# Masked softmax on one core: the transfer of the lengths behind an iota, and two waits on GpSimd moved

## The chip, the core and the metric

The kernel runs on one core of a Trainium2 chip. A core has five engines with instruction streams of their own: TensorE (PE, with its weight loads as PEld), VectorE (DVE), ScalarE (ACT), GpSimd (POOL) and SyncE (SP). They meet through semaphores: an instruction waits until a semaphore has reached a value, and raises one when it is done. Sixteen DMA engines move data between the chip's memory (HBM) and the on-chip buffer (SBUF). A transfer is issued by SyncE, ScalarE or GpSimd, and each of the three has its own DMA queue; the sixteen engines serve all queues.

The metric is the device time of one execution in microseconds (us), as the median of several runs. Beside it stands one profiled execution, whose trace gives the start and the end of each instruction.

## The reference

The input x has 16 batches of 8 heads with 256 x 256 float32 each. Every batch has a length between 128 and 255. Each row is a softmax over its first `length` columns; the columns behind it are zero.

```python
for b in range(batch):
    length = lengths[b]
    masked = x[b, :, :, :length].copy()
    masked = masked - np.max(masked, axis=-1, keepdims=True)
    exp_masked = np.exp(masked)
    result[b, :, :, :length] = exp_masked / np.sum(exp_masked, axis=-1, keepdims=True)
```

## The kernel before

A batch is 2048 rows of 256 columns, 2 MB. It lies in SBUF as 128 partitions with 16 rows each, and `xt` has eight such slots. The batches are worked through in sixteen positions; the first position is batch 1, and `batch_of` gives the batch of a position. A *half* is 8 of the 16 rows of each partition, 1 MB.

The work on one position runs through four engines. A load brings the batch into its slot. VectorE applies the mask to the columns from 128 on (`mask`, L248): the minimum of x and a bound that is hugely positive inside the length and hugely negative behind it. The bound is put together from two small tiles: `down`, made from a count of the columns (the *first bound*, L231), and `len_s`, the lengths of all batches on every partition (the *second bound*, L239). Both raise the semaphore `s_v`, so that `s_v` is 1 after the first and 2 after the second. ScalarE then takes the exponential in place (L374 for a quarter of the batch at once, L377 row by row with the sums). VectorE sums that quarter (`total`, L269), takes reciprocals (L279) and multiplies (`divide`, L282), half by half. SyncE stores the result in pieces (L154). The row's maximum is not subtracted; a check at the end (L317 to L328) would start a slow second pass if a sum were out of range.

VectorE's program interleaves two positions: after the first half of one has been divided it masks the next, then divides the second half and sums a quarter of the next. ScalarE runs through the slots in order.

The opening is this. GpSimd makes the count of the columns (`iota_i`, L181), a row and a column of ones, and two small memsets (`seed`) that raise the store semaphores. ScalarE issues the transfer of the sixteen lengths (L142) as its first act, then loads its table for the exponential (L361). SyncE issues the load of the first position in two halves (L145); VectorE masks each half when it has landed. VectorE makes the first bound when the iota is there, casts the lengths to `len_b` when they have landed (L236), TensorE spreads them over the partitions (L216), and VectorE makes the second bound from that (L239). GpSimd waits for `s_v` = 2 (L188). Then it fills the columns from 160 on of one slot with zeros (`fill(ahead)`, L191), issues the loads of positions 1 to 3 (L196), waits for the lengths, and fills three more slots.

Later loads are issued by GpSimd in a loop (L168), each only as wide as the length of its batch needs, in steps of eight columns, which is why slots have to be filled. Each waits for the store that frees its slot and for the last load but one.

A transfer's instruction stands in its engine's stream, and its packets go through that engine's DMA queue. SyncE's stores wait for the divided half (`s_out`), and from position 2 on also for the stores two positions earlier.

Of the kernel before, what the change touches and what calls it, by code (L numbers as in the profile page):

```python
# [21 lines left out]
def kernel(  # L22
# [6 lines left out]
    nc = tc.nc  # L29
# [20 lines left out]
    def batch_of(pos):  # L50
        return pos + 1 if pos < ahead - 1 else {ahead - 1: 15, 15: 0}.get(pos, pos)
# [54 lines left out]
    with tc.tile_critical(no_gpsimd_drain=True):  # L106
# [8 lines left out]
        s_iota = sem("s_iota")  # L115
        s_fill = sem("s_fill")
        s_v = sem("s_v")
# [21 lines left out]
            )  # L139


        nc.scalar.dma_start(out=word64, in_=lengths[None, :]).then_inc(s_word, 16)  # L142
        for h in range(2):
            s = slice(h * half, (h + 1) * half)
# [40 lines left out]
        nc.gpsimd.memset(ones_c, 1.0).then_inc(s_ones, 1)  # L185
        for par in range(2):
            nc.gpsimd.memset(seed[:, par : par + 1], 0.0).then_inc(s_st[par], 128)  # L187
        nc.gpsimd.wait_ge(s_v, 2)  # L188

        def fill(b):  # L190
            nc.gpsimd.memset(xt[:, b, :, low:], 0.0).then_inc(s_fill, 1)  # L191


        fill(ahead)
        for b in range(1, ahead):
            nc.gpsimd.dma_start(out=xt[:, b], in_=x_f[batch_of(b)]).then_inc(  # L196
                s_sw[b - 1] if b < 3 else s_ld[2], 16
            )
# [239 lines left out]
```

## Time and profile before

| what | value |
|---|---|
| median of 3 runs | 154.57 us (154.54 to 154.61) |
| span of the profiled execution | 152.8 us |
| VectorE busy | 134.6 us, 88% |
| ScalarE busy | 95.1 us, 62% |
| GpSimd busy | 21.3 us, 14% |
| moved by DMA | 61.57 MB, mean 403 GB/s |
| HBM read, written | 27.98 MB, 33.55 MB |

The span goes from the first to the last instruction of the profiled execution; the run's time takes in what lies around it. Busy times are those of instructions on an engine: an issue by SyncE or ScalarE isn't counted. In the lists that follow, L142 is line 142 of the kernel before; a row of the timeline gives the start from the span's beginning, the duration, the engine (with a q where the engine's sequencer issues a transfer), the line, the operation, what is written and what is read, and in brackets how long the engine stood idle and what ended that. A packet counts in the window in which it starts, which is why a share can be somewhat above 1 or 100%.

### The profile page before, as it was taken

Reading aid. Unit: us, or ns where it says so; the run is one execution under the profiler, and the core shown is the slowest. Engines: PE = TensorE matmul, PEld = TensorE weight load, DVE = VectorE, ACT = ScalarE, POOL = GpSimd, SP = SyncE. Lnnn points to the kernel's source line nnn. Section 1 sums busy time; section 2 is a strip of 40 time slices with the busy share of each in tenths; the row PEclk is TensorE's granted clock in tenths of the full one; section 3 lists DMA queues with packets and bytes.
Section 4 is the critical chain, followed back from the end, with each engine's and each line's share of the span. In section 5 each row is a group of like instructions: output and inputs, shape, how many; then the busy total and the mean of one; then the engine's idle time right before and its main releaser. Section 6 shows DMA issues by size and latency. Waiting matters only on the chain.

```text
span 152.8 us, 818 instructions
## 1 busy us (share of the span) xinstructions
PE 0.3 (0%) x2; PEld 0.2 (0%) x2; DVE 134.6 (88%) x107; ACT 95.1 (62%) x402; POOL 21.3 (14%) x29
## 2 busy tenths in 40 slices
PE   0000000000000000000000000000000000000000
PEld 0000000000000000000000000000000000000000
DVE  1369999999999999999999999999999999999500
ACT  3096699339394967859393939577593939395000
POOL 4962110030303020030300220302000000000000
DMA  4999999999999999999999999999999999999994
GB/s 107 420 446 433 401 435 347 421 445 420 394 397 422 405 421 411 411 409 405 419 411 418 408 399 419 408 410 423 417 421 419 413 420 422 435 435 442 429 410 187
DMA packets 10646, 61.57 MB, mean 403 GB/s; under 512 B 898, under 2 KB 1010, under 8 KB 7058
## 3 DMA queue, kind: packets, MB, share of 16 engines
q1 hardware_dynamic: 5904, 35.65, 56.7%
q0 software_dynamic: 4736, 25.89, 41.9%
q14 instruction: 4, 0.03, 0.1%
q10 hardware_dynamic: 2, 0.00, 0.0%
HBM read 27.98 MB, written 33.55 MB: 403 GB/s over the span
## 4 chain that ended last, share of the span: by engine, by line
DVE 87%; DMA 5%; issue 1%; SPq 0%; PE 0%
DVE xt L282 48%; DVE xt L248 23%; DVE row_sum L269 12%; DMA xt<-in_x_dram 5%; DVE inv_sum L279 3%; DVE ends L317 0%; SPq L145 0%; DVE bad L320 0%; PE count L218 0%; DVE redo L328 0%; SPq L433 0%; SPq L106 0%
## 5 line engine op out<-in xcount | busy, mean ns | idle before, releaser
L377 ACT ACTIVATE xt<-xt 128x256 f32<-128x256 f32 x192 | 76.6, 400 | 0.2 <-DVE xt L248 0.2
L282 DVE TENSOR_TENSOR xt<-xt,inv_sum 128x2048 f32<-128x2048 f32 x32 | 73.3, 2292 | 1.1
L374 ACT ACTIVATE xt<-xt 128x1024 f32<-128x1024 f32 x16 | 16.9, 1056 | 42.8 <-DVE xt L248 42.8
L248 DVE SCALAR_TENSOR_TENSOR xt<-down,len_s,xt 128x2048 f32<-128x2048 f32 (+1 forms) x17 | 37.7, 2219 | 5.0 <-DMA xt<-in_x_dram 5.0
L377 ACT ACTIVATION_READ_ACCUMULATOR xt<-xt 128x1 f32 x192 | 35.9, 187 | 0.0
L168 POOL DMA_DIRECT2D xt<-in_x_dram x12 | 13.2, 1104 | 84.0 <-DMA xt<-in_x_dram 62.3
L269 DVE TENSOR_REDUCE row_sum<-xt 128x4 f32<-128x1024 f32 x16 | 19.4, 1210 | 0.0
L279 DVE RECIPROCAL inv_sum<-row_sum 128x8 f32<-128x8 f32 x32 | 6.3, 198 | 0.5
L191 POOL MEMSET xt<- 128x1536 f32 x4 | 5.4, 1398 | 1.1 <-DVE len_s L239 1.1
L361 ACT ACT_TABLE_LOAD x1 | 1.3, 1283 | 1.6 <-SPq L106 1.6
L196 POOL DMA_DIRECT2D xt<-in_x_dram x3 | 1.8, 590 | 0.0
L231 DVE TENSOR_SCALAR down<-iota_i 128x256 f32<-128x256 int32 x1 | 0.3, 300 | 1.6 <-POOL iota_i L181 1.6
L317 DVE TENSOR_REDUCE ends<-inv_sum 128x1 f32<-128x256 f32 x2 | 0.7, 408 | 0.0
L236 DVE CAST len_b<-word 1x16 bf16<-1x16 int32 x1 | 0.2, 164 | 0.4 <-DMA word<-in_lengths_dram 0.4
L239 DVE TENSOR_SCALAR len_s<-len_f 128x16 f32<-128x16 f32 x1 | 0.2, 176 | 0.3 <-PE len_f L216 0.3
L218 PE MATMUL count<-bad,ones_c 128*1 128x3 bf16 x1 | 0.2, 165 | 140.8 <-DVE bad L320 140.8
L181 POOL IOTA iota_i<- 128x256 int32 x1 | 0.3, 331 | 0.6 <-SPq L106 0.6
L328 DVE TENSOR_REDUCE redo<-count 1x1 f32<-1x3 f32 x1 | 0.1, 150 | 0.3 <-PE count L218 0.3
L320 DVE TENSOR_SCALAR bad<-ends 128x1 bf16<-128x1 f32 x3 | 0.3, 150 | 0.0
L187 POOL MEMSET seed<- 1x1 f32 x2 | 0.2, 225 | 0.0
L218 PEld LDWEIGHTS count<-bad,ones_c 128*1 128x1 bf16 x1 | 0.1, 79 | 140.8 <-DVE bad L320 140.8
L361 ACT ACTIVATE warm<-const-float32-0.0 128x1 f32<-128x1 f32 x1 | 0.2, 204 | 0.0
(10 smaller groups left out, 1.1 us busy)
## 6 DMA issues: line engine op xcount, KB each, us to landing
out_dram<-xt SPq DMA_DIRECT2D x20, 1024.0 KB
xt<-in_x_dram POOLq DMA_DIRECT2D x4, 2048.0 KB, 16.3
out_dram<-xt SPq DMA_DIRECT2D x15, 512.0 KB
xt<-in_x_dram POOLq DMA_DIRECT2D x3, 1728.0 KB, 16.7
out_dram<-xt SPq DMA_DIRECT2D x2, 2048.0 KB
xt<-in_x_dram POOLq DMA_DIRECT2D x2, 1600.0 KB, 16.0
xt<-in_x_dram POOLq DMA_DIRECT2D x2, 1280.0 KB, 14.7
xt<-in_x_dram SPq DMA_DIRECT2D x2, 1024.0 KB, 6.4
```

The source lines that it names most:

```text
L168: nc.gpsimd.dma_start(out=xt[:, slot, :, :w], in_=x_n[:, b, :, :w]).then_inc(s_sw[par], 16)
L191: nc.gpsimd.memset(xt[:, b, :, low:], 0.0).then_inc(s_fill, 1)
L196: nc.gpsimd.dma_start(out=xt[:, b], in_=x_f[batch_of(b)]).then_inc(s_sw[b - 1] if b < 3 else s_ld[2], 16)
L218: nc.tensor.matmul(count, lhsT=ones_c, rhs=bad, start=True, stop=True).then_inc(s_count, 1)
L248: return nc.vector.scalar_tensor_tensor(out=t, in0=down[:, None, lo:hi].to_broadcast([P, s.stop - s.start, hi - lo]), scalar=len_s[:, batc ...
L269: nc.vector.tensor_reduce(out=row_sum[:, b % slots, :lump], in_=xt[:, b % slots, :lump, :], op=ALU.add, axis=AX,).then_inc(s_exp[0], 1)
L279: step(nc.vector.reciprocal(out=inv_sum[:, b, s], in_=row_sum[:, b % slots, s]))
L282: nc.vector.tensor_tensor(out=t, in0=t, in1=inv_sum[:, b, s, None].to_broadcast([P, half, seq_k]), op=ALU.mult,).then_inc(s_out, 1)
L317: step(nc.vector.tensor_reduce(out=ends[:, k : k + 1], in_=values, op=op, axis=AX))
L361: nc.scalar.activation(out=warm, in_=nc.const_aps.tensor(0.0, (P, 1), F32), func=EXP)
L374: nc.scalar.activation(out=e, in_=e, func=EXP).then_inc(s_lump, 1)
L377: ins = nc.scalar.activation(out=e, in_=e, func=EXP, accum_out=row_sum[:, slot, j : j + 1])
```

## The change

ScalarE waits for the iota before it issues the transfer of the lengths. GpSimd's wait for `s_v` = 2 is split: the first fill waits for `s_v` = 1, and the three loads behind it for `s_v` = 2. Nothing is added to or taken from the computation; the lines below the first added one move by one, those below the second by two.

```diff
+        nc.scalar.wait_ge(s_iota, 1)
         nc.scalar.dma_start(out=word64, in_=lengths[None, :]).then_inc(s_word, 16)
...
             nc.gpsimd.memset(seed[:, par : par + 1], 0.0).then_inc(s_st[par], 128)
-        nc.gpsimd.wait_ge(s_v, 2)
+        nc.gpsimd.wait_ge(s_v, 1)

         def fill(b):
             nc.gpsimd.memset(xt[:, b, :, low:], 0.0).then_inc(s_fill, 1)


         fill(ahead)
+        nc.gpsimd.wait_ge(s_v, 2)
         for b in range(1, ahead):
             nc.gpsimd.dma_start(out=xt[:, b], in_=x_f[batch_of(b)]).then_inc(
                 s_sw[b - 1] if b < 3 else s_ld[2], 16
             )
```

## The prediction

> **What bounds the kernel now.** I read the page first: which engine is busy, what the DMA queues took, and the chain that ended last.
>
> ```profile
> span 152.8 us, 818 instructions
> ...
> q1 hardware_dynamic: 5904, 35.65, 56.7%
> q0 software_dynamic: 4736, 25.89, 41.9%
> ...
> DVE 87%; DMA 5%; issue 1%; SPq 0%; PE 0%
> ```
>
> Two things claim the time. The chain names VectorE (DVE), 87%. But the two data queues together took 56.7 + 41.9 = 98.6% of what sixteen DMA engines have in the whole span. And the shares of the chain add up to some 93%, so it doesn't reach the end. The chain in order of time shows where it stops:
>
> ```profile
> 1.58 7.66 DMA xt<-in_x_dram
> ...
> 143.74 0.15 DVE redo L328
> ```
>
> It stops at 143.89, 8.9 us before the span does. So I read the busy share of the DMA engines stage by stage (columns: stretch, length, busy time of PE, PEld, DVE, ACT, POOL, clock, DMA share, GB/s), and what SyncE waited for at the end:
>
> ```profile
> 1.00:2.17 1.17, 0.00 (x0) 0.00 (x0) 0.30 (x1) 0.52 (x1) 0.70 (x5) 1.00 0.00 0
> 2.17:3.40 1.23, 0.17 (x1) 0.10 (x1) 0.34 (x2) 0.96 (x2) 0.35 (x1) 1.00 1.13 240
> 3.40:8.46 5.06, 0.00 (x0) 0.00 (x0) 1.28 (x1) 0.68 (x1) 5.06 (x6) 1.00 1.00 421
> 8.46:126.50 118.04, 0.00 (x0) 0.00 (x0) 115.83 (x85) 82.23 (x352) 14.95 (x14) 1.00 1.02 413
> 126.50:142.46 15.96, 0.00 (x0) 0.00 (x0) 15.75 (x13) 10.71 (x50) 0.00 (x0) 1.00 1.02 433
> 142.46:151.30 8.84, 0.17 (x1) 0.08 (x1) 1.14 (x7) 0.00 (x0) 0.00 (x0) 1.00 0.93 393
> ```
>
> ```profile
> SPq L433 <- DMA out_dram<-xt: 4.2, 1, 4.2
> ```
>
> Nothing moves before 2.17; then the DMA engines are full until about 151, and SyncE's last act is to wait 4.2 us for a store. The kernel is a DMA pipe of 149 us that is never empty, with VectorE almost as full beside it. So a microsecond in which the DMA engines stand idle comes back at the end, and a late VectorE costs nothing while stores are queued. How much may it be late? After the last store has been issued (142.83) the store queue still moves this much, in the view of the DMA queues:
>
> ```profile
> q1 hardware_dynamic: 379, 3.33, 78.6%
> ```
>
> 3.33 MB less the last store's own 1.05 is 2.28 MB of older stores, at 433 GB/s 5.3 us of slack.
>
> The change touches the opening, so that is what I read next, in order of time (start, duration, instruction, idle time before it). First ScalarE's issue and the first of SyncE's two, then VectorE, then GpSimd, and the first store:
>
> ```profile
> 1.09 0.52 ACTq L142 DMA_DIRECT2D word<-in_lengths_dram  x1
> 1.14 0.39 SPq L145 DMA_DIRECT2D xt<-in_x_dram  x1
> ```
>
> ```profile
> 1.61 0.30 DVE L231 TENSOR_SCALAR down<-iota_i 128x256 f32<-128x256 int32 x1 [1.61 <-POOL iota_i L181]
> 2.31 0.16 DVE L236 CAST len_b<-word 1x16 bf16<-1x16 int32 x1 [0.40 <-DMA word<-in_lengths_dram]
> 2.82 0.18 DVE L239 TENSOR_SCALAR len_s<-len_f 128x16 f32<-128x16 f32 x1 [0.35 <-PE len_f L216]
> 6.46 1.28 DVE L248 SCALAR_TENSOR_TENSOR xt<-down,len_s,xt 128x1024 f32<-128x1024 f32 x1 [3.47 <-DMA xt<-in_x_dram]
> ...
> 14.16 2.34 DVE L248 SCALAR_TENSOR_TENSOR xt<-down,len_s,xt 128x2048 f32<-128x2048 f32 x1
> ```
>
> ```profile
> 3.05 1.39 POOL L191 MEMSET xt<- 128x1536 f32 x1 [1.11 <-DVE len_s L239]
> 4.37 1.76 POOL L196 DMA_DIRECT2D xt<-in_x_dram  x3
> ```
>
> ```profile
> 14.27 0.34 SPq L154 DMA_DIRECT2D out_dram<-xt  x1
> ```
>
> And the DMA queues in short windows: q1 is SyncE's queue, q10 ScalarE's, q0 GpSimd's, and a row gives packets, MB, share. From 1.98 to 2.00 come the lengths' two packets, 0.89 us after their issue at 1.09:
>
> ```profile
> q10 hardware_dynamic: 2, 0.00, 6.2%
> ```
>
> From 2.17 to 5.20 SyncE's queue runs alone and moves nearly the whole first half of x:
>
> ```profile
> q1 hardware_dynamic: 119, 0.97, 99.4%
> ```
>
> From 4.30 to 7.66 it is still alone, though GpSimd issued its first load at 4.37:
>
> ```profile
> q1 hardware_dynamic: 188, 1.41, 99.4%
> ```
>
> From 7.66 to 8.46 GpSimd's packets come in as the two halves run out, and from 8.46 to 9.30 the last two, small packets of the halves follow:
>
> ```profile
> q0 software_dynamic: 20, 0.33, 95.5%
> q1 hardware_dynamic: 24, 0.08, 25.1%
> ...
> q1 hardware_dynamic: 2, 0.00, 0.1%
> ```
>
> From 14.20 to 17.90 GpSimd's queue is alone, though SyncE issued its store at 14.27:
>
> ```profile
> q0 software_dynamic: 107, 1.57, 103.7%
> ```
>
> And GpSimd's first load lands 9.3 us after its issue, at 13.7:
>
> ```profile
> xt<-in_x_dram POOLq DMA_DIRECT2D x1, 2048.0 KB, 9.3
> ```
>
> So in both places where one queue was running and another began, the newcomer's packets waited: 3.3 us (4.37 to 7.66) and 3.6 us (14.27 to 17.90), where an issue into idle engines took 1.03 us (1.14 to 2.17).
>
> **The change part by part.** *The lengths.* ScalarE's issue moves from 1.09 to when the iota is done. VectorE's first bound waits for the same iota and starts at 1.61, so I take 1.61. Behind the wait on ScalarE stand its table load and the exponentials, which need nothing before the first mask at 6.46: a delay of 0.52 there is hidden. Unhindered, the lengths would be cast 1.22 us after the issue, as now (1.09 to 2.31): at 2.83. But their packets would come at 1.61 + 0.89 = 2.50, and by then (from 2.17) the DMA engines are in the first half of x. No row shows so small a transfer in a busy engine. Bounds: it overtakes, cast at 2.83; or it waits until both halves are out at 8.46, and with the 0.32 from packets to cast (1.99 to 2.31) the cast is at 8.78. I take the middle case, nearest to the two newcomers above: it waits for about what is queued when it comes, the first half of x, out at 5.2, and the cast starts at 5.5.
>
> *The fill.* It moves ahead, behind the first bound, which ends at 1.91: from about 2 to 3.4 in place of 3.05 to 4.44. VectorE and the DMA engines don't need it; its 1.39 us is hidden behind the wait for the lengths, and no longer stands ahead of the loads. If that cover were gone it would delay the loads by at most these 1.39.
>
> *The loads.* They now wait for the second bound: the cast plus 0.69 (2.31 to its end at 3.00) plus 0.05 (3.00 to GpSimd at 3.05). With the cast at 5.5: issued at 6.24 in place of 4.37, 1.87 later. Behind them on GpSimd stand three more fills and the later loads, first needed at 14.5.
>
> *Does that leave the DMA engines idle?* How soon GpSimd's load reaches an idle engine isn't shown. From below: its issue, 1.76 / 3 = 0.59 (SyncE's took 0.39), and then what SyncE's needed from its issue's end at 1.53 to 2.17, 0.64: together 1.23. From above: the 3.30 that it took behind the halves. I take the middle, 2.3, which also pays for the slow start that 240 GB/s against 421 in the rows shows. So its packets come at 6.24 + 2.3 = 8.54. The halves run out between 7.66 and 8.46, on the mean at 8.06. Idle: 0.48 us on the mean engine. By the lower bound, 7.47, none; by the upper, 9.54, 1.48.
>
> [...]
>
> *The halves.* They no longer have the lengths' issue just ahead of theirs. The lengths took 0.89 from issue to packets, the first half 1.03; if all of the difference is waiting, 0.14 is won, if none, 0. I take 0.07. VectorE's later second bound is hidden: done at 6.2, the first mask starts at 6.46.
>
> *Sum:* 152.8 + 0.48 - 0.07 = 153.2. The runs' median of 154.57 lies 1.77 above the span, which I leave as it is: 154.57 + 0.41 = 154.98, forecast 155.0, slower. Its own range is 154.5 (no idle time) to 156.0 (1.48).
>
> **The rivals.** *The lengths overtake (not slower).* If the engines serve the lengths' one packet between two of x, the cast starts soon after 2.83, the fill is over at 3.4, and the loads go out at 3.6 to 4.2, ahead of 4.37. No engine idles, and the time is that of before less the 0.07: 154.5. The load's packets would then come in among the last of the second half and delay its landing, but the VectorE that waits for it has 5.3 us of slack. It decides if the cast comes before about 5.0, where the idle time is gone. For it: the transfer is one packet on one engine. Against it: both newcomers above waited over 3 us. [...]
>
> *The lengths wait for both halves.* Cast at 8.78, loads at 9.52, their packets at 11.8: 3.8 us idle, 158.3. VectorE's first mask would slip from 6.46 to 9.5, inside its slack. For it: GpSimd's load came in only as the halves ran out. Against it: the lengths arrive before most of the second half is queued.
>
> *VectorE is the bound after all, and it gains.* If the chain is right and the end hangs on VectorE, the second half's landing at 9.24 counts. Two of its small packets came after 8.46, behind GpSimd's; with those loads later they would come sooner. The next mask, at 14.16, can't start before GpSimd's first load lands at 13.7, so at most 0.5 is won; I take 0.4: 154.2, faster. It decides only if the slack of 5.3 us is in truth nothing; against it are the stores that run on behind the chain's end at 143.89.
>
> **How the numbers follow.** Forecast 0.55, the lengths overtake 0.27, wait for both halves 0.08, VectorE gains 0.10. Predicted is the forecast's 155.0. The range is 154.2 to 156.2: from the VectorE case below to the upper bound of the idle time, with a little over for a later cast; the wait for both halves stays out. 0.2% is 0.31 us, about what a measurement of this kernel can tell from no change. Faster: 0.08 of the VectorE case and 0.04 of the overtaking one (which would need more than the 0.14) = 0.12. Slower: the wait for both halves and 0.46 of the forecast (idle time over 0.38) = 0.54. Within 0.2%: the rest, 0.34.
>
> **What would show it.** Step by step: the issue of the lengths at about 1.6; the cast at about 5.5 (near 3 if they overtake, near 8.8 if they wait for both halves); the first fill at 2.0; the loads at about 6.2. Then, in the DMA windows between 7.6 and 9, a share well under 1.00, and after it full engines and the last packet of the stores some 0.4 later than 151.3. That VectorE has slack shows if its end at 143.89 moves otherwise than the span does. The prediction is wrong if the cast comes early, if GpSimd's load is at the engines by 7.6, or if the end follows VectorE.

## The result, and the profile after

| | before | after |
|---|---|---|
| median of the runs | 154.56 us (8 runs) | 155.61 us (8 runs) |
| span of the profiled execution | 152.8 us | 153.8 us |

The change makes the kernel slower: the ratio is 1.007, 95% interval 1.0058 to 1.0083, or 1.05 us.

The page of the changed kernel, from the same places as before:

```profile
span 153.8 us, 818 instructions
...
q1 hardware_dynamic: 5904, 35.65, 56.4%
q0 software_dynamic: 4736, 25.89, 42.0%
...
DVE 84%; DMA 8%; issue 1%; PE 0%; POOL 0%; POOLq 0%; SPq 0%
```

The same bytes and the same packets take the same share of a longer span. The chain now gives 8% to the DMA engines; its order of time shows which transfers these are (start, duration, what):

```profile
1.61 4.06 DMA word<-in_lengths_dram
...
6.68 8.21 DMA xt<-in_x_dram
...
144.53 0.15 DVE redo L330
```

The lengths take 4.06 us from their issue to their landing, and the cast follows at 5.69; from issue to cast it is 4.08, where it was 1.22. GpSimd's first load is issued behind them and lands at 14.89. VectorE's work ends at 144.68, 0.79 later than before, and again 9 us ahead of the span's end. The timeline of the opening:

```profile
1.61 0.51 ACTq L143 DMA_DIRECT2D word<-in_lengths_dram  x1
...
1.97 1.39 POOL L192 MEMSET xt<- 128x1536 f32 x1
...
5.69 0.16 DVE L238 CAST len_b<-word 1x16 bf16<-1x16 int32 x1 [3.78 <-DMA word<-in_lengths_dram]
...
6.20 0.17 DVE L241 TENSOR_SCALAR len_s<-len_f 128x16 f32<-128x16 f32 x1 [0.35 <-PE len_f L218]
...
6.68 1.76 POOL L198 DMA_DIRECT2D xt<-in_x_dram  x3 [3.33 <-DVE len_s L241]
...
14.92 2.35 DVE L250 SCALAR_TENSOR_TENSOR xt<-down,len_s,xt 128x2048 f32<-128x2048 f32 x1 [1.30 <-DMA xt<-in_x_dram]
```

Everything stands in the order of the prediction: issue at 1.61, fill out of the way at 1.97, cast at 5.69, loads at 6.68 in place of 4.37. In the view of the DMA queues the lengths' two packets come from 5.15 to 5.17, and GpSimd's queue has no packet until 8.09 and these until 8.60:

```profile
q10 hardware_dynamic: 2, 0.00, 6.9%
...
q0 software_dynamic: 13, 0.21, 211.7%
```

What the DMA engines make of it is in the stretches (the last two columns are DMA share and GB/s):

```profile
2.15:3.40 1.25, 0.00 (x0) 0.00 (x0) 0.00 (x0) 1.24 (x1) 1.21 (x1) 1.00 1.08 242
3.40:7.54 4.14, 0.17 (x1) 0.10 (x1) 1.47 (x3) 0.24 (x2) 0.86 (x2) 1.00 0.97 410
7.54:8.10 0.56, 0.00 (x0) 0.00 (x0) 0.15 (x1) 0.37 (x1) 0.56 (x2) 1.00 0.55 205
8.10:10.00 1.90, 0.00 (x0) 0.00 (x0) 1.36 (x2) 1.90 (x8) 1.90 (x3) 1.00 0.94 233
10.00:144.68 134.68, 0.17 (x1) 0.08 (x1) 131.47 (x102) 91.22 (x393) 15.71 (x14) 1.00 1.02 417
144.68:152.30 7.62, 0.00 (x0) 0.00 (x0) 0.00 (x0) 0.00 (x0) 0.00 (x0) 1.00 0.89 378
152.30:153.80 1.50, 0.00 (x0) 0.00 (x0) 0.00 (x0) 0.00 (x0) 0.00 (x0) 1.00 0.00 0
```

Here is the loss, and it has two parts. From 7.54 to 8.10 the halves run out and nothing follows: 205 GB/s, share 0.55. From 8.10 to 10.00 GpSimd's packets are there and keep the engines "busy" at 0.94, but they move 233 GB/s, where the same stretch of the kernel before moves 435:

```profile
8.10:10.00 1.90, 0.00 (x0) 0.00 (x0) 0.74 (x1) 1.90 (x8) 1.90 (x2) 1.00 1.02 435
```

These packets stay open longer: GpSimd's first sixteen took 1.32 us on the mean in the packet records of this trace, and 0.61 in that of the kernel before. Why, no view shows. Against the 435 the first part loses 0.56 x 230 / 435 = 0.30 us, the second 1.90 x 202 / 435 = 0.88, together 1.18, a little more than the 1.05 measured. After that the engines stay full, and the last packets are out at about 152, 1.0 later than before. So of two DMA columns the share alone would have shown a third of the loss.

### The profile page after: what moved, and what is told of

Read it like the earlier page. It is cut to its first block, busy times and chain, and to the rows that moved or that the text cites. A ratio compares the mean times of both kernels' runs of the same rounds, so it can differ in the third digit from the quotient of the medians.

```text
span 153.8 us, 818 instructions
## 1 busy us (share of the span) xinstructions
PE 0.3 (0%) x2; PEld 0.2 (0%) x2; DVE 134.8 (88%) x107; ACT 95.0 (62%) x402; POOL 21.3 (14%) x29
## 4 chain that ended last, share of the span: by engine, by line
DVE 84%; DMA 8%; issue 1%; PE 0%; POOL 0%; POOLq 0%; SPq 0%
DVE xt L284 46%; DVE xt L250 22%; DVE row_sum L271 11%; DMA xt<-in_x_dram 5%; DVE inv_sum L281 3%; DMA word<-in_lengths_dram 3%; DVE ends L319 0%; POOL iota_i L182 0%; DVE bad L322 0%; DVE len_s L241 0%; PE count L220 0%; PE len_f L218 0%; DVE len_b L238 0%; DVE redo L330 0%; POOLq L435 0%
```

## The experiments

Theory A is the prediction's: the DMA engines are the pipe that sets the end, and a late VectorE has slack. Theory B is the chain's: the end follows VectorE, which started its second position 0.76 later (14.16 to 14.92) and ended 0.79 later. B can explain most of the 1.05 too, so it had to be put to the test.

**Each part of the change alone.** GpSimd's waits as changed, the lengths issued first as before (the edit is against the changed kernel):

```diff
-        nc.scalar.wait_ge(s_iota, 1)
         nc.scalar.dma_start(out=word64, in_=lengths[None, :]).then_inc(s_word, 16)
```

> GpSimd's two waits as in the change, ScalarE's issue of the lengths first as before. Expected start of GpSimd's loads 3.3 to 3.8 us, about 0.7 earlier than the 4.37 of before. Theory A (the DMA engines are the pipe that sets the end, VectorE has slack): no idle time, 154.4 to 154.7. Theory B (VectorE's chain sets the end): the loads' packets come in among the last of the second half, which lands 1 to 2 us later than 9.24, and the end moves with it: 155.5 to 156.5.

Measured: 154.56 us, ratio 0.9995 (0.9985 to 1.0004). The loads did not go out at 3.3 to 3.8 but at 4.22, and the timeline of this kernel shows why:

```profile
1.97 1.39 POOL L191 MEMSET xt<- 128x1536 f32 x1
2.31 1.07 DVE L237 CAST len_b<-word 1x16 bf16<-1x16 int32 x1 [0.40 <-DMA word<-in_lengths_dram]
...
4.22 1.76 POOL L197 DMA_DIRECT2D xt<-in_x_dram  x3 [0.86 <-DVE len_s L240]
```

The cast starts on time but takes 1.07 us in place of 0.16: it ends at 3.38, with the fill (3.36). So the fill was not won; it is in the way on another engine. With the loads at 4.22, A and B lie too near each other here, and the run says only that the split costs nothing.

The other part alone, the kernel before with ScalarE's wait, so that GpSimd's fill and loads both stay behind the second bound:

```diff
+        nc.scalar.wait_ge(s_iota, 1)
         nc.scalar.dma_start(out=word64, in_=lengths[None, :]).then_inc(s_word, 16)
```

> ScalarE's wait for the iota alone; GpSimd's fill and loads both behind the second bound as before. The cast at about 5.7 as in the changed kernel, the fill from about 6.4 to 7.8, the loads at about 7.8, 1.1 later than the 6.68 of the changed kernel. Theory A: 1.1 us more without packets, 156.7. Theory B: GpSimd's first load lands 1.1 later, the mask behind it too, 156.4 to 156.7. A third theory, that the split of the waits itself costs time, gives less than 155.6.

Measured: 157.07 us, ratio 1.0158 (1.0143 to 1.0174). The cast came at 6.26, the loads at 8.32, and the stretches show the hole bare:

```profile
8.00:9.70 1.70, 0.00 (x0) 0.00 (x0) 1.36 (x2) 1.40 (x4) 1.70 (x4) 1.00 0.00 0
9.70:11.50 1.80, 0.00 (x0) 0.00 (x0) 1.73 (x4) 1.80 (x10) 1.80 (x3) 1.00 0.96 209
```

1.7 us without a byte, then 1.8 us at half rate. So ScalarE's wait carries the whole loss, and the split takes back more than half of it, because the fill then lies in the wait for the lengths. Of the 1.64 by which the loads are later than in the changed kernel, 0.57 is a cast that came later in this execution (6.26 against 5.69), though the lengths were issued at the same time in both.

**The late loads, or the late lengths?** The changed kernel with its loads no longer behind the second bound:

```diff
         fill(ahead)
-        nc.gpsimd.wait_ge(s_v, 2)
         for b in range(1, ahead):
```

> The changed kernel with its loads no longer behind the second bound: cast still at about 5.7, loads at about 3.4 behind the fill. Theory A: all of the loss is gone and the 0.1 us by which the first half runs ahead is left: 154.4 to 154.6. Theory B: the second half lands 1 to 2 us later than 9.24, 155.5 to 156.5. If the late lengths themselves cost the time: 155.6 as in the changed kernel.

Measured: 154.80 us, ratio 1.0015 (1.0005 to 1.0024). It is theory A's side, with 0.2 us more than expected, and it came with a large surprise on VectorE (timeline, and landing of the second half from the view of the issues):

```profile
3.29 1.76 POOL L197 DMA_DIRECT2D xt<-in_x_dram  x3
5.64 4.07 DVE L237 CAST len_b<-word 1x16 bf16<-1x16 int32 x1 [3.73 <-DMA word<-in_lengths_dram]
5.66 4.02 POOL L192 MEMSET xt<- 128x1536 f32 x3 [0.61 <-DMA word<-in_lengths_dram]
...
146.33 0.15 DVE L329 TENSOR_REDUCE redo<-count 1x1 f32<-1x3 f32 x1 [0.26 <-PE count L219]
```

```profile
xt<-in_x_dram SPq DMA_DIRECT2D x1, 1024.0 KB, 9.7
```

The cast takes 4.07 us, the second half, now sharing the engines with GpSimd's load, lands 9.7 us after its issue in place of 7.7, and VectorE ends at 146.48, 2.6 us later than before. Yet the time moves by 0.2. Theory B falls with this run.

The fills were the suspects for the slow cast, so the next kernel keeps them away from it, behind the second bound:

```diff
-        nc.gpsimd.wait_ge(s_word, 16)
+        nc.gpsimd.wait_ge(s_v, 2)
         for b in range(ahead + 1, slots):
             fill(b)
```

> The kernel with the loads not behind the second bound, and the three later fills behind that bound in place of behind the landing of the lengths. In the version with the loads free the cast took 4.07 us and ended with those three fills (5.66 to 9.68). If the fills hold the cast up, it takes 0.16 here, and VectorE's end comes earlier than the 146.5 there by up to 2 us. If something else does (the late lengths, the DMA engines), the cast stays at some 4 us. Time by theory A: 154.5 to 154.8 either way.

Measured: 154.72 us, ratio 1.0009 (1.0000 to 1.0018).

```profile
6.21 0.16 DVE L237 CAST len_b<-word 1x16 bf16<-1x16 int32 x1 [4.30 <-DMA word<-in_lengths_dram]
...
6.95 4.03 POOL L192 MEMSET xt<- 128x1536 f32 x3 [1.91 <-DVE len_s L240]
```

Back to 0.16: the fills held the cast. VectorE still ended at 146.0, since the second half landed late. The 0.1 us by which the first half should run ahead does not show in the time.

**How much slack VectorE has.** The kernel before with useless VectorE instructions behind the second mask, one and then three (a range of 3 in the second kernel); they write into a tile that nothing reads:

```diff
         mask(0, slice(half, nt))
+        for k in range(1):
+            d = down[:, None, :].to_broadcast([P, half, seq_k])
+            nc.vector.tensor_tensor(out=spare[:, k], in0=d, in1=d, op=ALU.min)
```

> The kernel before with one more VectorE instruction behind the second mask, a minimum of 2048 columns into a tile that nothing reads, 2.3 us. Theory A: inside VectorE's 5.3 us of slack, 154.5 to 154.8. Theory B: 154.6 + 2.3 = 156.9.

Measured: 154.72 us, ratio 1.0009 (1.0000 to 1.0019). In the timeline the added instruction stands at 10.55, and VectorE's last work is 2.3 us later than before:

```profile
10.55 2.29 DVE L294 TENSOR_TENSOR spare<-down 128x2048 f32<-128x2048 f32 x1
...
146.04 0.15 DVE L332 TENSOR_REDUCE redo<-count 1x1 f32<-1x3 f32 x1 [0.26 <-PE count L219]
```

2.3 us on the engine that the chain of waits calls critical cost 0.1.

> The kernel before with three such VectorE instructions of 2.3 us, 6.9 us together. Theory A: 6.9 less the 5.3 us of slack, 156.2; and the DMA engines show idle time only near the end. Theory B: 161.5.

Measured: 157.03 us, ratio 1.0149 (1.0129 to 1.0170). The timeline and the stretches near the end:

```profile
150.36 0.15 DVE L332 TENSOR_REDUCE redo<-count 1x1 f32<-1x3 f32 x1 [0.26 <-PE count L219]
```

```profile
139.00:140.00 1.00, 0.00 (x0) 0.00 (x0) 1.00 (x1) 0.00 (x0) 0.00 (x0) 1.00 1.11 475
140.00:144.00 4.00, 0.00 (x0) 0.00 (x0) 3.96 (x4) 3.48 (x14) 0.00 (x0) 1.00 0.33 139
144.00:148.00 4.00, 0.00 (x0) 0.00 (x0) 3.90 (x5) 2.36 (x12) 0.00 (x0) 1.00 0.93 393
```

VectorE ends 6.62 us later (143.89 to 150.51), the kernel 2.48: the slack is 4.1 us, where the prediction had 5.3. When it is used up, the stores run dry between 140 and 144, ahead of the last store but two, which is issued at 142.95. (From position 13 on a store no longer waits for those two positions earlier, L152, so that stores can queue up at the end.)

**The late loads alone, with the lengths early.** The kernel before with two, then three fills ahead of GpSimd's loads in place of one (+ 2, then + 3, and the later fills begin there):

```diff
-        fill(ahead)
+        for b in range(ahead, ahead + 2):
+            fill(b)
```

> The kernel before with two fills ahead of GpSimd's loads in place of one: loads at 4.37 + 1.35 = 5.7 with the lengths still early. In the changed kernel the first packets came 1.41 after the issue (6.68 to 8.10), so here at 7.1, just before the halves run out at 7.66. Theory A: no or little idle time, 154.5 to 154.9. Theory B: the second half lands up to 0.4 sooner, 154.2 to 154.5.

Measured: 155.47 us, ratio 1.0061 (1.0042 to 1.0081). Neither theory had this. The loads went out at 5.87, and the stretches and the DMA queues from 7.58 to 8.00 show packets that were there in time and yet slow:

```profile
8.00:10.00 2.00, 0.00 (x0) 0.00 (x0) 1.30 (x2) 2.00 (x8) 2.00 (x2) 1.00 0.91 324
10.00:12.00 2.00, 0.00 (x0) 0.00 (x0) 1.93 (x3) 2.00 (x11) 0.33 (x1) 1.00 1.00 426
```

```profile
q0 software_dynamic: 8, 0.13, 129.3%
```

GpSimd's packets come in as the halves run out, with no hole worth the name. But they move 324 GB/s for two microseconds, where the kernel before moves 438: 2.00 x 114 / 438 = 0.52 us. So it wasn't enough here that the load's packets came in as the halves ran out. In the kernel before, issued 3.3 us ahead of their first packet, they ran at the 438 from the first on; issued 1.7 ahead, at the 324. The 0.92 us of this run is more than the 0.52. The rest shows at the end, in the stretch from 151 to 152 of the kernel before and of this one:

```profile
151.00:152.00 1.00, 0.00 (x0) 0.00 (x0) 0.00 (x0) 0.00 (x0) 0.00 (x0) 1.00 0.00 0
151.00:152.00 1.00, 0.00 (x0) 0.00 (x0) 0.00 (x0) 0.00 (x0) 0.00 (x0) 1.00 0.24 98
```

Up to 148 us this kernel has moved 0.18 MB less, 0.44 us at 413 GB/s. Then the work runs out more slowly: the DMA share is 0.89 from 150 to 151 and 0.24 from there to 152, where the kernel before has 0.72 and 0.00. Why it ends so here is open.

> The kernel before with three fills ahead of GpSimd's loads: loads at 7.07, packets at 8.5, lengths still early. Theory A: as in the changed kernel and 0.4 later still, without the 0.1 by which its halves run ahead: 155.6 + 0.5 = 156.1. Theory B: GpSimd's first load lands at about 15.3, the mask behind it 1.1 later than 14.16, 155.7. If it is the late lengths and not the late loads that cost the time: 154.6.

Measured: 155.97 us, ratio 1.0085 (1.0068 to 1.0102). The loads went out at 7.01:

```profile
7.01 1.75 POOL L197 DMA_DIRECT2D xt<-in_x_dram  x3
```

The lengths were as early as ever, and the kernel is slower than the changed one: it is the loads' lateness that costs, whatever makes them late.

How slow the first packets are goes with the time from the issue of the load to its first packet. GpSimd's first sixteen packets took 0.61 us on the mean after 3.3 us (the kernel before), 1.07 after 1.7 (two fills), and 1.32 and 1.35 after 1.4 (the change and three fills). One rival stands untested: in the slow cases a mask of VectorE ran beside the issue of these loads (6.41 to 7.69 beside 6.68 to 8.44 in the changed kernel), in the kernel before none did. What the loss is made of inside the engines is therefore open; that the late loads cause it is not.

**What the lengths wait for.** The changed kernel with ScalarE behind the first fill, when both halves have long been issued:

```diff
-        nc.scalar.wait_ge(s_iota, 1)
+        nc.scalar.wait_ge(s_fill, 1)
```

> The changed kernel with ScalarE's issue behind the first fill in place of the iota, at about 3.4, 1.8 later, when both halves have long been issued. If the lengths wait for all that has been issued before them: packets after 7.6, cast at about 8.2, loads at 9.2, 158. If they wait for what a DMA engine holds at a time, some 2.4 us of packets: cast at about 7.0, loads at 8.0, 156.9. If they take turns packet by packet: cast at about 5.0, loads at 6.0, 154.9.

Measured: 157.46 us, ratio 1.0186 (1.0165 to 1.0206). The view of the DMA queues has one packet of the lengths in 6.75 to 6.76 and the other in 7.065 to 7.075; the cast and the loads follow in the timeline:

```profile
q10 hardware_dynamic: 1, 0.00, 8.1%
...
q10 hardware_dynamic: 1, 0.00, 5.6%
```

```profile
7.45 0.16 DVE L238 CAST len_b<-word 1x16 bf16<-1x16 int32 x1 [5.54 <-DMA word<-in_lengths_dram]
...
8.45 1.75 POOL L198 DMA_DIRECT2D xt<-in_x_dram  x3 [5.10 <-DVE len_s L241]
```

The issue was at 3.38, so by an estimate, with the 0.89 from issue to packets of the kernel before, the lengths were there at 4.27. They neither came in at once (cast at 5.0 expected) nor behind all of both halves (after 7.6): they waited 2.5 us, near the 2.4 of the middle case. In the changed kernel 125 packets of x began ahead of the lengths, some eight for each of the sixteen engines; at 0.31 us, the median of the 8 KB packets there, eight are 2.5 us, an estimate. That a DMA engine holds so many no run shows. Nor was it the end of the first half, which is out by about 5.2: they came in the middle of the second. Their second packet, one of 4 bytes behind the 128, came 0.31 later. The wait differs between executions: with the issue at 1.6, so by the same estimate there at 2.5, the packets came at 5.15 in the changed kernel and at 5.10, 5.64 and 5.69 in the kernels with the loads free, with the fills behind, and with ScalarE's wait alone. That is 2.6 to 3.2 us. Does the wait go by a number of packets, or by bytes? The changed kernel with the first half in two loads, so that its packets are half as large:

```diff
-        for h in range(2):
-            s = slice(h * half, (h + 1) * half)
+        for h, s in ((0, slice(0, quarter)), (0, slice(quarter, half)), (1, slice(half, nt))):
             nc.sync.dma_start(out=xt[:, 0, s], in_=x_f[batch_of(0), :, s]).then_inc(s_ld[h], 16)
...
             if b == 0:
-                nc.vector.wait_ge(s_ld[s.start // half], 16)
+                nc.vector.wait_ge(s_ld[s.start // half], 16 if s.start else 32)
```

> The changed kernel with the first half loaded as two quarters, in packets of 4 KB in place of 8. If a DMA engine has a number of packets taken up ahead of a newcomer (8 or 9), the lengths come after 8 small packets: packets at about 3.9, cast at 4.3, loads at 5.3, 154.6. If it has a number of bytes or a time taken up, or the lengths wait for all that was issued before: packets at about 5.2, cast at 5.6, time as the changed kernel's 155.6.

Measured: 156.55 us, ratio 1.0127 (1.0109 to 1.0146). The lengths' packets came from 4.31 to 4.33, the cast at 4.82, the loads at 5.81; then the stretches:

```profile
q10 hardware_dynamic: 2, 0.00, 6.9%
```

```profile
4.82 0.16 DVE L237 CAST len_b<-word 1x16 bf16<-1x16 int32 x1 [2.91 <-DMA word<-in_lengths_dram]
```

```profile
10.00:12.00 2.00, 0.00 (x0) 0.00 (x0) 1.93 (x4) 2.00 (x11) 1.59 (x2) 1.00 0.99 401
12.00:14.00 2.00, 0.00 (x0) 0.00 (x0) 2.00 (x1) 1.94 (x10) 0.00 (x0) 1.00 0.99 401
```

With half-size packets the lengths come 0.84 earlier (4.31 against 5.15 in the changed kernel), a wait of 1.8 us, below all of those behind 8 KB packets. That points at a number of packets rather than at bytes. The kernel before points the other way: its first store, behind GpSimd's 16 KB packets, came 3.6 us after its issue, and less the 1.03 of an issue into idle engines it waited 2.6, no longer than the lengths behind 8 KB. So whether the wait goes by packets or by bytes is open. The first quarter is out by 4.31 too, so that a wait for the first transfer as a whole would look the same here; the run before, where the lengths got in between the packets of the second half, speaks against that. The time is a miss: 156.55 where 154.6 was expected. From 10 to 14 the engines are full, but at 401 GB/s (434 and 426 in the kernel before). Up to 148 us this kernel has moved 0.40 MB less than the kernel before, 0.97 us at 413 GB/s; the other microsecond is again a drawn-out end, with a DMA share of 0.32 from 151.5 to 152 and of 0.09 from there to 153.5. Why is open. The start of its GpSimd load was hardly slow: the first sixteen packets came 2.2 us after the issue and took 0.68 us on the mean.

**The late loads in a row**, by the start of GpSimd's loads in the profiled run; the times are medians of all runs:

```
loads issued at   time, us   above its own before   what moved them
3.29              154.80     +0.18                  loads free
3.29              154.72     +0.14                  loads free, fills behind
4.22              154.56     -0.06                  split alone
4.37              154.56      0                     (the kernel before)
5.81              156.55     +1.97                  lengths behind two quarters
5.87              155.47     +0.92                  two fills
6.68              155.61     +1.05                  the change
7.01              155.97     +1.42                  three fills
8.32              157.07     +2.45                  ScalarE's wait alone
8.45              157.46     +2.91                  lengths behind the fill
```

From 6.68 on each microsecond of lateness costs about one: 6.68 to 8.32 is 1.64, and the time grows by 1.40. Whether the lengths or the fills make the loads late makes no difference that shows here. The quarters fall out of the row: their opening load is another, and half of their loss is the drawn-out end. No kernel here beats the one before: the split alone equals it, and the versions with the loads free are 0.1 and 0.2 us above it.

## Why the prediction came out as it did

The direction and the order of events were right, and so was the path: lengths late, loads late, engines short of work, a later end. The size was under half of what was measured, 0.41 against 1.05, and that it was not further off is partly luck. With the measured issue and arrival the prediction's own sum has next to no idle time: packets at 8.10, halves out at 8.06. It had a loss to show because it let the loads go out 0.44 too early and their packets need 0.88 too long.

- *The bound.* Right. The DMA engines are full from the opening to the last store; VectorE 2.3 and 2.6 us later costs 0.1 to 0.2. The slack was sized from the stores still queued at the end: 5.3 us predicted, 4.1 measured. The prediction took the stores queued at the last store; the queue runs dry earlier. When the last store but two has been issued in the kernel before (136.34 to 136.71), SyncE's queue still moves 5.95 MB, of which the last three stores are 4.19. The other 1.76 are 4.1 us at 433 GB/s. The rival in which VectorE is the bound fell with these runs.
- *The lengths wait behind x.* That they wait is right, from the two newcomers in the trace, and the cast came at 5.69 where 5.5 was predicted. That it came so near is partly luck. The prediction let them wait for the first half of x; issued 1.8 later they came in the middle of the second, after about as long a wait. And in two other executions with the issue at 1.6 the cast came at 6.21 and 6.26. The rival in which they overtake fell with this row, and the one in which they wait for both halves too. How a DMA engine chooses between two queues no run shows. Once both queues run, packets of both come in the same stretch: where the loads were free, 14 of GpSimd's and 5 of SyncE's from 7.1 to 7.5, and the second half landed 9.7 us after its issue in place of 7.7.
- *From the cast to the loads.* 0.74 predicted, 0.99 measured (5.69 to 6.68). The 0.05 us by which GpSimd followed the second bound was that of a memset; the issue of a transfer started 0.31 after the bound was done. With the cast this puts the loads 0.44 later than predicted.
- *From the loads to full engines.* This term failed most. The first packets came at 8.10, 1.42 after the issue, faster than the 2.3 assumed, near the lower bound of 1.23. But the 2.3 was to pay for the slow start as well, and it didn't: 1.9 us at 233 GB/s lose 0.88 us. The prediction looked for idle engines and priced 0.48, where 0.30 was lost before the first packets; most of the loss is packets that took longer (1.32 us in place of 0.61), and those count as busy time in the profile (a share of 0.94).
- *The halves run ahead.* The 0.07 was of no weight; with the loads free it didn't show.
- *The fill hidden.* In the changed kernel it is. That it would cost at most its 1.39 without cover is about what came: ScalarE's wait alone, which puts it ahead of the loads again, is 1.46 slower than the whole change, though a part of that is the later cast of its execution.

## What to carry to other kernels

Before you believe the chain of waits, see whether it reaches the end of the span, and add up the DMA queues' shares: VectorE made up nearly all of it here from 9.26 to its end at 143.89, 87% of the span, and had 4.1 us of slack. Where the DMA engines are the pipe, look at how long before its first packet a load is issued (here 3.3 us went with 438 GB/s, and 1.7 with 324), and at GB/s rather than the share of busy time (0.91 at the 324). A small transfer that other loads depend on is worth trying ahead of the large ones: here it took 1.22 us from issue to cast there, and 4.08 when issued half a microsecond later.

## What the runs showed of the hardware that was not expected

A cast of sixteen numbers on VectorE (int32 to bf16) took 0.16 us alone, 1.07 beside one GpSimd fill and 4.07 beside three. Each time it ended with the fills: at 3.38 with the one at 3.36 (the split alone), at 9.71 with the three at 9.68 (the loads free), though there the cast's row begins 0.02 us ahead of theirs. With the three fills behind the second bound it took 0.16 again. Masks of VectorE beside the same fills took their usual 1.28 (at 6.27 in the split alone, at 6.93 with the fills behind). Why the cast is held up and the masks are not, no run shows.

A transfer of 128 bytes that came to DMA engines busy with 8 KB packets of another queue waited 2.5 to 3.2 us, counted from an arrival estimated as 0.89 us after its issue. GpSimd's load, coming in as or after the halves had run out, moved 233 GB/s in its first 1.9 us (the change) and 209 in its first 1.8 (ScalarE's wait alone), half of the 435 of the kernel before, where it had been issued 3.3 us ahead of its first packet.
